# A hybrid decoder layer on one core: decode's weighted sum over value pages moved to TensorE, weight remainders to VectorE, key and value pages in separate rings

## The chip, the core and the metric

The kernel runs on one core of a Trainium2 chip. Its engines run side by side, each in its own program order: TensorE (PE, with its weight loads PEld), VectorE (DVE), ScalarE (ACT), GpSimd (POOL) and SyncE (SP), which here issues most loads. The metric is the device time of one execution in microseconds, the median of several runs; lower is better.

## The reference

One layer of a decoder, for a prompt of 512 tokens (after 16 meta tokens) and 8 decode sequences of one new token each with 2048 past tokens. All of it is fp32.

```
z = rmsnorm(h) @ w_in                       # 2048 -> 8192: hq hf hi hg | aq ak av ag, 8 heads of 128 each
o_hg = hgrn2_chunked(hq, 1-f, hi, log f)    # 8 heads, 128x128 state, chunks of 64; decode: one step on state_hgrn
o_at = diff_attend(aq, ak, av)              # w = softmax(q1 k1) - lam softmax(q2 k2), T5 bias, causal; o = w v
decode: k_past = cache_k[page_table]; v_past = cache_v[page_table]      # 16 pages of 128 tokens per sequence
mixed = concat(rmsnorm(o_hg)*silu(hg), 0.8*rmsnorm(o_at)*silu(ag))
y = rmsnorm(h + mixed @ w_out)              # 2048 -> 2048
```

Outputs are y for prompt and decode tokens, the new keys and values, and the HGRN states. For decode attention each sequence has, per page, 128 tokens by 8 heads by 128 values; `o[h, d]` is the sum over all 2048 tokens of `w[t, h] * v[t, h, d]`.

## The kernel before

**Dense stream.** The two projections are 80 blocks of 128 output features: 64 of `w_in` in the order aq, ak, av, then hi, hf, hq head by head, then the gates hg and ag, and 16 of `w_out` (the blocks o). A block is four groups of four contraction chunks. fp32 is built from two rounded parts: `split` (line 276) makes the high part `hi` of a group's weights on ScalarE and the exact remainder `lo = raw - hi` on POOL, or for some groups on VectorE (`lo_on_dve`, line 291); `group` (line 294) then issues hi x xh, hi x xl and lo x xh for both halves of the columns. The split runs three groups ahead of the products, in rings of four `hi` and four `lo`.

**Order of issue.** Each engine issues in the order of the program's text as it is run in Python (lines 1223 to 1230), and that order is decided there: after each group comes a *slot* (line 1173), in which every chain that can go on issues one stage (`step_threads`): prompt attention, the HGRN heads, the norms, decode's softmax. `fill` (line 559) then adds half passes over decode's pages until VectorE's planned time is a fixed lead ahead of TensorE's (`LATE`: 3.0, 1.5, 4.0 and 4.0 us by phase). The planned times come from `Clock` and `Counted` (lines 74 to 145), rough costs per instruction, among them when a load should have landed.

**Decode attention.** A page is 128 tokens (partitions) by 1024 (8 heads of 128). `page_step` (line 613) does half of a page's pass: for a key page one product with the query row `qb` on all partitions, and a sum over every 64 elements into the scores `scd`; for a value page four of eight products per half, `acc[:, h, :] += v[:, h, :] * w[:, g, h]` (SCALAR_TENSOR_TENSOR, 128x128 each), all on VectorE. Keys run three sequences ahead of values (`KA`), and then key and value pages alternate in one list `steps`, in one ring of six buffers (`pg`) that HGRN's decode state `sd` and values `vb` share. `load_pages` (line 595) issues page loads on SP: it reads the page's number, then starts the DMA, waiting for the buffer. `softmax_dec` (line 657) makes the weights `wd`. `pv_end` (line 694) sums `acc` over the partitions by eight products with a column of ones into `t_o`, and ScalarE copies it to `oSa`.

**End of decode.** Before the last gate block goes on, a loop (lines 1181 to 1185) issues whatever page steps are left.

Of the kernel before, what the change touches and what calls it, by code (L numbers as in the profile page):

```python
# [30 lines left out]
H = 8  # L31
# [6 lines left out]
W = 656                # period of the bias row: a strip's 528 columns and 127 rows  # L38
# [9 lines left out]
def shape_constants():  # L48
    """Matrices that depend on the shapes alone."""
# [8 lines left out]
    # one-hot rows of buckets (row 32: masked) for: the prompt's bias row, decode's far, near and new keys  # L58
# [15 lines left out]
class Clock:  # L74
    """Rough times at which the engines finish what has been issued, for the order of issue."""

    LATENCY = 0.15

    def __init__(self):
        self.now = dict.fromkeys(("pe", "dve", "act", "pool", "dma"), 0.0)  # L80
        self.written, self.read = {}, {}
        self.rings = {}

# [13 lines left out]
    def issue(self, e, cost, outs, ins):  # L97
        start = self.now[e]
        for table, aps in ((self.written, ins + outs), (self.read, outs)):
            for ap in aps:  # L100
                t, by = table.get(ap.tensor.name, (0.0, e))
                if by != e:
                    start = max(start, t + self.LATENCY)
        self.now[e] = end = start + cost
        for ap in ins:
# [5 lines left out]
    def arrive(self, ap, mb):  # L111
        """A load that is issued now."""
# [5 lines left out]
class Counted:  # L118
    """An engine whose instructions' rough times are kept."""
# [4 lines left out]
    def __getattr__(self, op):  # L124
        f = getattr(self.eng, op)

        def call(*a, **k):
# [6 lines left out]
            n = (ins[0] if op == "tensor_reduce" else outs[-1] if "out" not in k else outs[0]).free_size()  # L134
            if self.name == "pe":
                t = 0.11 if op == "transpose" else n / 2400 + 0.004 if ap_dtype(ins[0]) == F32R else 0.2 if n == 1 else max(0.11, n / 600)
            elif self.name == "dve":
                t = 0.065 + n / 960 + (0.06 if op in ("scalar_tensor_tensor", "tensor_tensor_reduce") else 0)
            elif self.name == "act":
                t = 0.07 + n / 1200  # L140
            else:
                t = n / 410
            self.clock.issue(self.name, t, outs, ins)
            return r
        return call

# [6 lines left out]
def layer_kernel(ctx: ExitStack, tc: tile.TileContext, A):  # L153
# [20 lines left out]
    def expln():  # L174
        """The table with both the exponential and the logarithm."""
# [53 lines left out]
    def keep_warm(n):  # L229
        """Products that nobody reads, for TensorE's clock."""  # L230
# [13 lines left out]
    blocks = []                 # (name, weights, halves of columns)  # L244
# [17 lines left out]
    LASTP = ((0, 256), (256, CQ))       # the last block in parts, so that little is left to store at the end  # L262
# [5 lines left out]
    def load_raw(i):  # L268
        """Half of a block's weights."""
# [6 lines left out]
    def split(u):  # L276
        """High part of a group of weights, rounded to float32r, and the exact rest."""
# [8 lines left out]
        (V if lo_on_dve(b, g) else G).tensor_tensor(lo, raw, hi.bitcast(F32), op=ALU.subtract)  # L286
# [3 lines left out]

    def lo_on_dve(b, g):
        return b == 1 or (0 < b < 8 and g % 2 == 0) or (b >= NIN and g == 1)
# [55 lines left out]
    # the norm's weights to every partition; to columns for the meta and decode tokens  # L348
# [34 lines left out]
    # the first block's first half runs while the rest of the prompt is transposed  # L383
# [46 lines left out]
    # the small parameters  # L430
# [34 lines left out]
    def small_constants():  # L465
# [15 lines left out]
        # the prompt's bias by distance, negated: a row per head, skewed through DRAM into a strip per head  # L481
# [31 lines left out]
    aq = mp.tile([P, H, CQ], F32, name="aq")            # -q/8, then the attention half of mixed  # L513
    ak = [None] * H
    hgm = [None] * H                                      # the HGRN half of mixed
# [9 lines left out]
    ktail = [cp.tile([P, 2 * NM], F32, name=f"kt{i}") for i in range(2)]     # the last keys of a head, its two parts apart  # L525
# [4 lines left out]
    # Each group of the dense product is followed by one stage of every chain that can go on; decode  # L530
    # attention's passes over pages fill VectorE up to the time that TensorE has reached.
# [27 lines left out]
    def fill():  # L559
        """Passes over pages until VectorE's work reaches to TensorE's present time."""  # L560
        ph = 0 if "av0" not in flags else 1 if "attn7" not in flags else 2 if "hgrn7" not in flags else 3
        while clock["dve"] < clock["pe"] + LATE[ph]:
            i = done[0]
            if i < len(loaded) and clock.written[loaded[i].tensor.name][0] > clock["pe"] + SOON:
# [4 lines left out]
    def later(slots, **k):  # L569
        """A store some slots from now, so that its queue's engine needn't wait."""  # L570
# [14 lines left out]
    for s in range(NS):  # L585
        ks = [("k", s + KA, g) for g in range(NPG)] if s + KA < NS else []
        vs = [("v", s, g) for g in range(NPG)]
        if s:
            steps += ks[:2] + [x for i in range(NPG) for x in vs[i:i + 1] + ks[i + 2:i + 3]]
        else:  # L590
            steps += vs[:2] + [x for i in range(NPG) for x in ks[i:i + 1] + vs[i + 2:i + 3]]
    loaded = []
    done = [0]

    def load_pages(upto):
        while len(loaded) < min(upto, len(steps)):
            kind, s, g = steps[len(loaded)]
            i = s * NPG + g
            t = pg.tile([P, H * P], F32, name="pgt", tag="pg", bufs=NPB)
            r = nc.sync.value_load(ptab[0:1, i:i + 1], min_val=0, max_val=NPHYS - 1)  # L600
            load(out=t, in_=(ck if kind == "k" else cv)[bass.ds(r, 1), :, :].rearrange("o t c -> (o t) c"))
            loaded.append(t)
            clock.arrive(t, 0.5)
# [3 lines left out]
    def load_q(s):  # L607
        if s < NS:
            qbs[s] = pg.tile([P, H * P], F32, name="qb", tag="acc" if s == 1 else "qb")
# [3 lines left out]
    def page_step():  # L613
        """Half of a page's pass."""
        i = done[0]
        if i >= len(steps):
            return False
        kind, s, g = steps[i]
        z = half[0]
        if z == 0:  # L620
            if kind == "k" and (flags.get("q", slot[0]) >= slot[0] or g == 0 and s >= KA and f"w{s - KA}" not in flags):
                return False
            if kind == "v" and (f"w{s}" not in flags or g == 0 and s and flags.get(f"pv{s - 1}", slot[0]) >= slot[0]):
                return False
            load_pages(i + 1)
            if g == 0 and kind == "k":
                scs[s] = sm.tile([P, NPG + 1, 2 * H], F32, name="scd", bufs=KA)
            elif g == 0:
                accs[s] = pg.tile([P, H, P], F32, name="acc", tag="acc")
        pt = loaded[i]  # L630
        if kind == "k":
            if z == 0:
                V.tensor_tensor(pt, pt, qbs[s], op=ALU.mult)
            else:
                V.tensor_reduce(scs[s][:, g, :], pt.rearrange("p (a d) -> p a d", d=64), axis=AX.X, op=ALU.add)
        else:
            acc, w = accs[s], ws[s]
            vt = pt.rearrange("p (h d) -> p h d", d=P)
            for h in range(z * H // 2, (z + 1) * H // 2):
                if g == 0:  # L640
                    V.tensor_scalar(acc[:, h, :], vt[:, h, :], w[:, g, h:h + 1], None, op0=ALU.mult)
                else:
# [614 lines left out]
```

## Time and profile before

| | us |
|---|---|
| median of 3 runs | 1352.16 (1349.47 to 1352.70) |
| span of the profiled execution, first to last instruction | 1346.6 |
| TensorE busy | 1218.8 (91%) |
| VectorE busy | 946.8 (70%) |
| POOL busy | 590.0 (44%) |
| ScalarE busy | 545.0 (40%) |
| DMA moved | 261 MB, 194 GB/s on average |

The page gives the profiled execution's span alone; the three runs were timed 2.9 to 6.1 us above it. Dense products are short and follow each other closely, and an instruction's duration holds the time through the array, so the sum of durations in a group of matmuls is more than the time they take up. All instructions issued through the planner's wrapper have the line of that wrapper (L128), so groups are told apart by tile names: `lo<-raw,hi` is a weight remainder, `ps` the dense products, `pgt` a page, `acc` the value sum, `ho` and `am` an HGRN head, `sc` attention scores, `t_o` the end of a sequence's value sum.

### The profile page before, as it was taken

What the parts mean: (1) busy time and instruction counts of PE and PEld (TensorE: products, weight loads), DVE (VectorE), ACT (ScalarE), POOL (GpSimd) and SP (SyncE); (2) the same over time, 40 slices, a digit from 0 to 9 for tenths busy, and PEclk for the clock granted to TensorE, in tenths of its full rate; (3) what the DMA queues carried; (4) which work ended last, traced back from release to release, by engine and by line L of the source; (5) the groups of instructions that cost most, each with busy time, mean ns of one, the idle gap of its engine ahead of it and who ended that gap; (6) DMA issues with size and microseconds to landing.
All of it is one profiled execution on the core that took longest, in us unless ns stands there. A gap on an engine that the chain in (4) does not pass through costs nothing. (4 is left out here: it accounts for less than half of the span.)

```text
span 1346.6 us, 25420 instructions
## 1 busy us (share of the span) xinstructions
PE 1218.8 (91%) x9260; PEld 1150.8 (85%) x9260; DVE 946.8 (70%) x1945; ACT 545.0 (40%) x1286; POOL 590.0 (44%) x415
## 2 busy tenths in 40 slices
PE   8999999999999999889979897989973849999995
PEld 6999999887787999789979897889973849999995
DVE  7410899977787879989999999999996544222123
ACT  6322232365566635445535443434310115232233
POOL 3123455422222434345343442534789684344350
PEclk9999999999999999899998998979986969999998
DMA  6453899844544567677786768769676532732323
GB/s 214 121 137 99 304 351 308 281 154 143 150 144 141 187 190 236 217 247 227 233 261 223 241 211 259 237 208 297 205 244 202 179 111 87 232 92 79 95 79 128
DMA packets 240961, 261.05 MB, mean 194 GB/s; under 512 B 8783, under 2 KB 198962, under 8 KB 240171
## 3 DMA queue, kind: packets, MB, share of 16 engines
q1 hardware_dynamic: 57298, 164.09, 36.3%
q10 hardware_dynamic: 183538, 95.34, 25.0%
q8 instruction: 73, 1.20, 0.4%
q14 instruction: 52, 0.43, 0.1%
HBM read 245.94 MB, written 16.14 MB: 195 GB/s over the span
## 5 line engine op out<-in xcount | busy, mean ns | idle before, releaser
L128 POOL TENSOR_TENSOR lo<-raw,hi 128x512 fp32r<-128x512 f32 x288 | 477.3, 1663 | 693.3 <-ACT hi L128 546.6
L128 PE MATMUL ps<-xh,hi 128*128 128x264 f32 (+2 forms) x2048 | 555.3, 300 | 9.1 <-ACT hv L128 5.7
L128 PE MATMUL ps<-xl,hi 128*128 128x264 f32 (+2 forms) x2048 | 535.6, 290 | 1.1 <-DVE xl L128 1.1
L128 PEld LDWEIGHTS ps<-xh,hi 128*128 128x128 f32 x2048 | 398.5, 195 | 26.3 <-issue 9.9
L128 PEld LDWEIGHTS ps<-xl,hi 128*128 128x128 f32 x2048 | 398.6, 195 | 5.2 <-issue 3.8
L128 PE MATMUL ps<-xh,lo 128*128 128x264 f32 (+2 forms) x2048 | 341.6, 290 | 43.5 <-POOL lo L128 43.5
L128 DVE SCALAR_TENSOR_TENSOR acc<-pgt,wd,acc 128x128 f32<-128x128 f32 x960 | 365.9, 452 | 0.0
L128 PEld LDWEIGHTS ps<-xh,lo 128*128 128x128 f32 x2048 | 292.8, 194 | 43.9 <-POOL lo L128 43.9
L128 ACT CAST hi<-raw 128x512 fp32r<-128x512 f32 x321 | 195.4, 616 | 291.2 <-PE ps L128 180.3
L128 DVE TENSOR_TENSOR pgt<-pgt,qb 128x1024 f32<-128x1024 f32 x128 | 172.4, 1347 | 38.4 <-DMA pgt<-in_cache_k 29.8
L128 DVE TENSOR_REDUCE scd<-pgt 128x16 f32<-128x1024 f32 x128 | 155.4, 1214 | 2.3
L128 PE MATMUL ps<-mh,hi 128*128 128x256 f32 (+1 forms) x512 | 130.0, 286 | 3.0 <-ACT gate L128 1.5
L128 PE MATMUL ps<-ml,hi 128*128 128x256 f32 (+1 forms) x512 | 128.5, 283 | 0.0
L128 PEld LDWEIGHTS ps<-mh,hi 128*128 128x128 f32 x512 | 96.4, 188 | 3.9 <-ACT gate L128 1.7
L128 PEld LDWEIGHTS ps<-ml,hi 128*128 128x128 f32 x512 | 96.5, 188 | 0.0
L128 DVE TENSOR_TENSOR lo<-raw,hi 128x512 fp32r<-128x512 f32 x33 | 34.8, 1059 | 79.7 <-ACT hi L128 79.3
L128 DVE TENSOR_TENSOR xr<-xr,t_y 128x512 f32<-128x512 f32 (+1 forms) x17 | 11.2, 656 | 112.3 <-PE t_y L128 112.3
L128 PE MATMUL ps<-mh,lo 128*128 128x256 f32 (+1 forms) x512 | 82.4, 283 | 0.0
L128 PEld LDWEIGHTS ps<-mh,lo 128*128 128x128 f32 x512 | 70.3, 188 | 0.0
L128 DVE SCALAR_TENSOR_TENSOR p<-p,r,p 128x144 f32<-128x144 f32 (+3 forms) x32 | 18.1, 566 | 41.6 <-ACT p L128 41.5
L128 ACT COPY hgm<-ho 128x128 f32<-128x128 f32 x32 | 8.5, 265 | 86.0 <-PE ho L128 86.0
L128 DVE TENSOR_SCALAR acc<-pgt,wd 128x128 f32<-128x128 f32 x64 | 21.4, 402 | 29.2 <-PE t_o L128 29.2
(227 smaller groups left out, 1214.0 us busy)
## 6 DMA issues: line engine op xcount, KB each, us to landing
pgt<-in_cache_k SPq DMA_DIRECT2D x128, 512.0 KB
pgt<-in_cache_v SPq DMA_DIRECT2D x128, 512.0 KB
raw<-in_w_in ACTq DMA_DIRECT2D x125, 512.0 KB
raw<-in_w_out ACTq DMA_DIRECT2D x32, 512.0 KB
x<-in_x_prompt SPq DMA_DIRECT2D x4, 1024.0 KB
qb<-qd SPq DMA_DIRECT2D x8, 512.0 KB
sd<-in_state_hgrn SPq DMA_DIRECT2D x8, 512.0 KB
vb<-hvd SPq DMA_DIRECT2D x8, 512.0 KB
```

What stands on the lines that cost most here:

```text
L128: r = f(*a, **k)
```

## The change

- Every weight remainder `lo` is computed on VectorE.
- The weighted sum over value pages is done by TensorE. A value step takes two pages. Four fp32 products, one for each half of each page, have 32 columns of weights as the stationary operand (the page's 8 heads and those of the pages behind it, of which only the first 8 rows of the result matter) and 512 columns of values as the moving one; they write PSUM partitions 0, 32, 64 and 96 of one bank `t_pv`. VectorE copies the first into `acc` and adds the other seven of a sequence. The wanted values lie in blocks on the diagonal; `pv_end` transposes `acc` in four parts and picks them with a strided read.
- Key pages have a ring of three (`kp`), value pages a ring of two (`pg`), `sd` and `vb` a buffer each. A value step is issued at most once per slot, when the planner thinks that both pages have landed; it then issues the loads of the next two.
- Keys may run two sequences ahead of the softmax and three ahead of the end of values.
- The planner's costs and latencies are others, and it knows a port that POOL and some VectorE instructions hold. Some small tiles share buffers. Comments and docstrings are gone.

```diff
 class Clock:
-    LATENCY = 0.15
+    LATENCY = 0.07
...
+    def port(self, t):
+        for a, b in self.held:
+            if a <= t < b:
+                t = b
+        return t
...
     def split(u):
...
-        (V if lo_on_dve(b, g) else G).tensor_tensor(lo, raw, hi.bitcast(F32), op=ALU.subtract)
+        V.tensor_tensor(lo, raw, hi.bitcast(F32), op=ALU.subtract)
...
-    NPB = 6                     # pages on chip
+    NKB, NPB = 3, 2
...
-    AHEAD = NPB - 1
-    KA = 3                      # sequences by which the keys run ahead of the values
-    steps = [("k", s, g) for s in range(KA) for g in range(NPG)]
...
+    VB = 2
+    NVB = NPG // VB
+    ksteps = [(s, g) for s in range(NS) for g in range(NPG)]
+    vsteps = [(s, n) for s in range(NS) for n in range(NVB)]
...
+    def load_values():
+        n = len(vloaded)
+        if n < len(vsteps):
+            s, m = vsteps[n]
+            vloaded.append([load_page(cv, s * NPG + m * VB + i, "pg", NPB) for i in range(VB)])
...
     def page_step():
...
-            if kind == "k" and (flags.get("q", slot[0]) >= slot[0] or g == 0 and s >= KA and f"w{s - KA}" not in flags):
+            if flags.get("q", slot[0]) >= slot[0] or g == 0 and (s >= 2 and f"w{s - 2}" not in flags or s >= KA and f"pv{s - KA}" not in flags):
                 return False
...
-            for h in range(z * H // 2, (z + 1) * H // 2):
-                if g == 0:
-                    V.tensor_scalar(acc[:, h, :], vt[:, h, :], w[:, g, h:h + 1], None, op0=ALU.mult)
-                else:
-                    V.scalar_tensor_tensor(acc[:, h, :], vt[:, h, :], w[:, g, h:h + 1], acc[:, h, :], op0=ALU.mult, op1=ALU.add)
...
+    def value_step(landed=True):
+        n = vdone[0]
+        if n >= len(vsteps) or n >= len(vloaded):
+            return
+        s, m = vsteps[n]
+        if flags.get(f"w{s}", slot[0]) >= slot[0] or m == 0 and s and flags.get(f"pv{s - 1}", slot[0]) >= slot[0]:
+            return
+        if landed and any(clock.written[t.tensor.name][0] > clock["pe"] for t in vloaded[n]):
+            return
+        po = tp("t_pv")
+        wb = [ws[s][:, m * VB + i:m * VB + i + 32 // H, :].rearrange("p g h -> p (g h)") for i in range(VB)]
+        for r in range(VB // 2):
+            for j in range(4):
+                i = 2 * r + j // 2
+                T.matmul(po[32 * j:32 * j + 32, :], wb[i], vloaded[n][i][:, j % 2 * 512:(j % 2 + 1) * 512],
+                         start=r == 0, stop=r == VB // 2 - 1)
+        if m == 0:
+            accs[s] = pg.tile([P, 512], F32, name="acc", tag="acc")
+            V.tensor_copy(accs[s], po)
+        else:
+            V.tensor_tensor(accs[s], accs[s], po, op=ALU.add)
+        vdone[0] += 1
+        load_values()
+        if m == NVB - 1:
+            spawn(pv_end(s))
...
     def pv_end(s):
...
-        for h in range(H):
-            T.matmul(t[:, h:h + 1], accs[s][:, h, :], ones[:, 0:1], start=True, stop=True)
-        S.copy(oSa[:, s, :], t[:, 0:H])
+        for c in range(4):
+            T.transpose(t[:, c * P:(c + 1) * P], accs[s][:, c * P:(c + 1) * P], ident)
+        parts_ = [bass.AP(tensor=t.tensor, offset=t.offset + o, ap=[list(t.ap[0]), [36, 2], [P + 1, 4]]) for o in (0, 64)]
+        V.tensor_copy(oSa[:, s, :].rearrange("p (a c) -> p a c", c=4), parts_[0])
+        V.tensor_tensor(oSa[:, s, :].rearrange("p (a c) -> p a c", c=4), oSa[:, s, :].rearrange("p (a c) -> p a c", c=4), parts_[1], op=ALU.add)
...
-        sd = pg.tile([P, NS, P], F32, name="sd", tag="pg", bufs=NPB)
+        sd = pg.tile([P, NS, P], F32, name="sd", tag="sd")
...
     for u in range(NG, (NB - 1) * NG):
...
         step_threads()
+        value_step()
         fill()
```

The instructions move as follows. On VectorE in the middle of an HGRN head, before (`am` and `st` are the head's, `pgt` with `scd` a key page, `acc` a value page's eight products):

```order
L128 TENSOR_REDUCE scd<-pgt 128x16
L128 SCALAR_TENSOR_TENSOR acc<-pgt,wd,acc 128x128 x8
L128 TENSOR_TENSOR pgt<-pgt,qb 128x1024
L128 COPY_PREDICATED am_500<-cst,at 128x128
L128 SCALAR_TENSOR_TENSOR st<-st,eb,up 128x128 x2
```

and in the changed program at such a place:

```order
L149 TENSOR_TENSOR lo<-raw,hi 128x512
L149 COPY_PREDICATED am_501<-cst,at 128x128
L149 SCALAR_TENSOR_TENSOR st<-st,eb,up 128x128 x2
L149 TENSOR_TENSOR acc<-acc,t_pv 128x512
L149 TENSOR_TENSOR pgt<-pgt,qb 128x1024
```

The eight products of a value page have gone from between two `am`; a remainder per group and an addition from PSUM per value step stand there.

At the end of decode on VectorE, before (the values of the last two sequences, then decode's norm):

```order
L128 TENSOR_SCALAR acc<-pgt,wd 128x128 x8
L128 SCALAR_TENSOR_TENSOR acc<-pgt,wd,acc 128x128 x120
L128 TENSOR_SCALAR acc<-pgt,wd 128x128 x8
L128 SCALAR_TENSOR_TENSOR acc<-pgt,wd,acc 128x128 x120
L128 TENSOR_TENSOR wnew<-wnew,avS 128x64
```

and in the changed program:

```order
L149 TENSOR_TENSOR lo<-raw,hi 128x512 x3
L149 TENSOR_TENSOR acc<-acc,t_pv 128x512
L149 TENSOR_TENSOR lo<-raw,hi 128x512 x2
L149 COPY oSa<-t_o 128x8
L149 TENSOR_TENSOR oSa<-oSa,t_o 128x8
```

The two runs of 120 products are gone; the last value steps come one every three groups of remainders.

On TensorE, the end of a sequence in an HGRN slot before (`ps` is the dense stream, `at` and `up` the head's):

```order
L128 MATMUL ps<-xh_109,lo 128x264 x4
L128 MATMUL at<-qe,hf 128x128
L128 MATMUL up<-hvtok,hktok 128x128 x2
L128 MATMUL t_o<-ones,acc 128x1 x8
L128 MATMUL ps<-xh_110,hi 128x272
```

and a value step in such a slot of the changed program:

```order
L149 MATMUL ps<-xh_109,lo 128x264 x4
L149 MATMUL at<-qe,hf 128x128
L149 MATMUL up<-hvtok,hktok 128x128 x2
L149 MATMUL t_pv<-pgt,wd 32x512 x4
L149 MATMUL ps<-xh_110,hi 128x272
```

There are 64 such steps, most of them two or three groups apart, the last 81 groups of dense products before the end; the last `t_o` of before stands 70 groups before the end.

## Rows read from the trace of the kernel before

**Rows 1.** The page's busy table and its slices (tenths, 40 slices).

```profile
PE 1218.8 (91%) x9260; PEld 1150.8 (85%) x9260; DVE 946.8 (70%) x1945; ACT 545.0 (40%) x1286; POOL 590.0 (44%) x415
...
PE   8999999999999999889979897989973849999995
```

**Rows 2.** Stages: busy us of each engine, granted clock, DMA share and rate.

```profile
440.00:935.00 495.00, 452.82 (x3389) 430.97 (x3388) 457.90 (x826) 230.22 (x566) 216.33 (x151) 0.94 0.73 231
935.00:1147.00 212.00, 157.20 (x1227) 155.57 (x1225) 143.57 (x447) 51.85 (x100) 156.99 (x69) 0.86 0.58 179
```

**Rows 3.** Waits of TensorE: us in total, times, longest.

```profile
PE ps L128 <- POOL lo L128: 43.5, 2, 22.4
PE ho L128 <- DVE am L128: 27.9, 13, 7.0
PE t_o L128 <- DVE acc L128: 9.6, 3, 7.5
PE t_hkt L128 <- DVE cf L128: 6.1, 3, 2.1
```

**Rows 4.** Timeline of POOL in the decode tail: start, duration, what.

```profile
999.85 32.91 POOL L128 TENSOR_TENSOR lo<-raw,hi 128x512 fp32r<-128x512 f32 x2 [1.83 <-ACT hi L128]
...
1039.72 1.28 POOL L128 TENSOR_TENSOR lo<-raw,hi 128x512 fp32r<-128x512 f32 x1 [1.85 <-ACT hi L128]
```

**Rows 5.** Timeline of VectorE there.

```profile
998.82 31.59 DVE L128 SCALAR_TENSOR_TENSOR acc<-pgt,wd,acc 128x128 f32<-128x128 f32 x120
...
1132.39 0.69 DVE L128 TENSOR_TENSOR lo<-raw,hi 128x512 fp32r<-128x512 f32 x1
```

**Rows 6.** VectorE in an HGRN head, without and with a remainder on POOL.

```profile
535.05 2.18 DVE L128 SCALAR_TENSOR_TENSOR acc<-pgt,wd,acc 128x128 f32<-128x128 f32 x8
...
539.53 3.18 DVE L128 SCALAR_TENSOR_TENSOR acc<-pgt,wd,acc 128x128 f32<-128x128 f32 x8
```

**Rows 7.** Four stretches at the lower clock, columns as in Rows 2.

```profile
1012.20:1036.10 23.90, 4.51 (x21) 4.51 (x22) 18.21 (x70) 1.24 (x2) 23.90 (x6) 0.50 0.71 226
1077.00:1097.50 20.50, 3.22 (x14) 3.22 (x15) 16.10 (x62) 1.14 (x2) 20.50 (x5) 0.50 0.33 104
541.10:551.40 10.30, 7.28 (x32) 6.83 (x33) 9.40 (x24) 2.53 (x8) 1.27 (x1) 0.50 0.67 229
...
821.00:827.80 6.80, 6.80 (x30) 6.35 (x31) 6.56 (x19) 2.54 (x8) 1.27 (x1) 0.50 0.78 275
```

**Rows 8.** Groups: xcount, busy us, mean ns of one, idle before.

```profile
L128 POOL TENSOR_TENSOR lo<-raw,hi 128x512 fp32r<-128x512 f32 x288 | 477.3, 1663 | 693.3 <-ACT hi L128 546.6 <-issue 77.2 <-PE ps L128 30.4
...
L128 DVE SCALAR_TENSOR_TENSOR acc<-pgt,wd,acc 128x128 f32<-128x128 f32 x960 | 365.9, 452 | 0.0
...
L128 DVE TENSOR_TENSOR lo<-raw,hi 128x512 fp32r<-128x512 f32 x33 | 34.8, 1059 | 79.7 <-ACT hi L128 79.3 <-ACT lbe L128 0.3
...
L128 DVE TENSOR_TENSOR xr<-xr,t_y 128x512 f32<-128x512 f32 x15 | 10.3, 688 | 104.5 <-PE t_y L128 104.5
```

**Rows 9.** Timeline of TensorE: scores, a norm's sum, a sequence's end.

```profile
264.09 1.13 PE L128 MATMUL sc<-ak,aq 64*128 64x512 f32 x4
265.14 0.41 PE L128 MATMUL se<-kt,aq 128*128 128x32 f32 x2
...
299.59 1.12 PE L128 MATMUL t_ra<-sq,ones 128*128 128x512 f32 x2
...
466.77 1.70 PE L128 MATMUL t_o<-ones,acc 128*128 128x1 f32 x14
```

**Rows 10.** The chain that ended last, two pieces of the output projection.

```profile
1164.98 0.44 PE t_y L128 x4
1165.52 11.50 PE ps L128 x96
```

**Rows 11.** Timeline of the load queue at the first key pages.

```profile
133.77 23.84 SPq L601 DMA_DIRECT2D pgt<-in_cache_k  x12
```

**Rows 12.** Timeline of VectorE at the first key page.

```profile
140.96 1.22 DVE L128 TENSOR_TENSOR pgt<-pgt,qb 128x1024 f32<-128x1024 f32 x1 [29.25 <-DMA pgt<-in_cache_k]
```

More of the change, by code (lines that the diff above doesn't have):

```diff
@@ L95, in tile, with issue @@
         return t
-    def issue(self, e, cost, outs, ins):
+    def port(self, t):
[3 more added lines that the diff above has]
+        return t
+    def issue(self, e, cost, outs, ins, latency=0.08, shared=False):
         start = self.now[e]
@@ L103, in issue @@
                     start = max(start, t + self.LATENCY)
+        if e == "pool":
+            start = self.port(start)
+            self.pool_held = start + cost
+        elif shared:
+            start = max(start, self.pool_held)
+            a, b = self.held[-1]
+            self.held = self.held[-40:]
+            if start - b < 0.03:
+                self.held[-1] = (a, start + cost)
+            else:
+                self.held.append((start, start + cost))
         self.now[e] = end = start + cost
+        end += latency
         for ap in ins:
@@ L133, in call @@
             ins = aps + [x for n, x in k.items() if hasattr(x, "free_size") and n not in ("out", "accum_out")]
-            n = (ins[0] if op == "tensor_reduce" else outs[-1] if "out" not in k else outs[0]).free_size()
+            n = max(ins[0].free_size(), 1) if op == "tensor_reduce" else (outs[-1] if "out" not in k else outs[0]).free_size()
+            late, shared = 0.08, False
+            from_psum = any(in_psum(x) for x in ins + outs)
+            wide = [x for x in ins if x.free_size() > 1 and not in_psum(x)]
@@ L135, in call @@
             if self.name == "pe":
-                t = 0.11 if op == "transpose" else n / 2400 + 0.004 if ap_dtype(ins[0]) == F32R else 0.2 if n == 1 else max(0.11, n / 600)
-            elif self.name == "dve":
-                t = 0.065 + n / 960 + (0.06 if op in ("scalar_tensor_tensor", "tensor_tensor_reduce") else 0)
+                late = 0.165
+                if op == "transpose":
+                    t = 0.11
+                elif ap_dtype(ins[0]) == F32R:
+                    t = max(0.11, n / 2400 + 0.0115)
+                else:
+                    t = 2 * max(0.118, n / 1200 + min(ins[0].free_size(), P) / 1200)
+                    if ins[0].partition_size() == 64:
+                        t /= 2
+                    if ins[0].free_size() == 32:
+                        t /= 4
+            elif self.name == "dve":
+                two = op in ("scalar_tensor_tensor", "tensor_tensor_reduce")
+                one = op in ("tensor_scalar", "tensor_copy") and not from_psum
+                t = (0.13 if two or op == "tensor_scalar" else 0.075) + n / (1920 if one else 960) * (2 if op == "tensor_tensor_scan" else 1)
+                if op == "tensor_tensor_reduce":
+                    t += 0.13
+                shared = len(wide) >= 2 or one and n > 64
@@ L139, in call @@
             elif self.name == "act":
-                t = 0.07 + n / 1200
+                t = n / 1200 + (0.055 if from_psum else 0.095) + (0.09 if hasattr(k.get("scale"), "free_size") or k.get("accum_out") is not None else 0)
             else:
-                t = n / 410
-            self.clock.issue(self.name, t, outs, ins)
-            return r
-        return call
+                t = 0.07 + n / 430
+            self.clock.issue(self.name, t, outs, ins, late, shared)
+            return r
@@ L148, in ap_dtype, with in_psum @@
+        return call
+def in_psum(ap):
+    return ap.space == bass.MemoryType.PSUM
 def ap_dtype(ap):
@@ L563, in fill @@
             i = done[0]
-            if i < len(loaded) and clock.written[loaded[i].tensor.name][0] > clock["pe"] + SOON:
+            if i < len(kloaded) and any(clock.written[t.tensor.name][0] > clock["pe"] + SOON for t in (kloaded[i], qbs[ksteps[i][0]])):
                 break
@@ L581, in layer_kernel, with load_page, load_keys @@
     scs, qbs, ws, accs = {}, {}, {}, {}
-    AHEAD = NPB - 1
-    KA = 3
-    steps = [("k", s, g) for s in range(KA) for g in range(NPG)]
[L585 to L589, printed above, removed]
-        else:
[L591 to L603, printed above, removed]
+    VB = 2
+    NVB = NPG // VB
+    ksteps = [(s, g) for s in range(NS) for g in range(NPG)]
+    vsteps = [(s, n) for s in range(NS) for n in range(NVB)]
+    kloaded, vloaded = [], []
+    done, vdone = [0], [0]
+    def load_page(src, i, tag, bufs):
+        t = pg.tile([P, H * P], F32, name="pgt", tag=tag, bufs=bufs)
+        r = nc.sync.value_load(ptab[0:1, i:i + 1], min_val=0, max_val=NPHYS - 1)
+        load(out=t, in_=src[bass.ds(r, 1), :, :].rearrange("o t c -> (o t) c"))
+        clock.arrive(t, 0.5)
+        return t
+    def load_keys(upto):
+        while len(kloaded) < min(upto, len(ksteps)):
+            kloaded.append(load_page(ck, len(kloaded), "kp", NKB))
+    def load_values():
[3 more added lines that the diff above has]
+            vloaded.append([load_page(cv, s * NPG + m * VB + i, "pg", NPB) for i in range(VB)])
     half = [0]
@@ L608, in load_q @@
         if s < NS:
-            qbs[s] = pg.tile([P, H * P], F32, name="qb", tag="acc" if s == 1 else "qb")
+            qbs[s] = pg.tile([P, H * P], F32, name="qb", tag="qb")
             clock.arrive(qbs[s], 0.5)
```

69 lines of the change are left out of this document (30 added, 39 removed).

## The prediction

> **What bounds the kernel now.** I read the page's busy table and slices first, then the stages, then TensorE's waits, then the timeline at the longest of them. TensorE is busy for 91% of the span and its slices stand at 8 or 9 but for one dip near the end [rows 1], so the time is TensorE's work, plus the holes in it, plus what its clock loses. The holes are few and have owners: two of 22 us each are TensorE waiting for a weight remainder `lo` from POOL (43.5 in all), and 27.9 + 9.6 + 6.1 = 43.6 us are waits for VectorE's results (`am`, `acc`, `cf`) [rows 3]. They lie where VectorE is fullest: between 440 and 935 us, the HGRN heads, it is busy for 458 of 495 us; the decode tail follows [rows 2].
>
> The two long holes are one mechanism. VectorE runs 120 products of value pages in a row, 31.59 us, and over the same stretch POOL takes 32.91 us for two remainders, of which one takes 1.28 alone [rows 4, 5]. A POOL instruction that reads SBUF does not get in between VectorE instructions with two SBUF inputs. The other way round one remainder on POOL stretches eight such products from 2.18 to 3.18 us [rows 6], and the product of scores, `am`, stands behind them. The Trainium skill (SBUF — State Buffer, Who interferes with whom) has the shared ports taken by whoever issues first, for one whole instruction. By that POOL would lose at most one product, 0.26 us, and the first term below would be nothing (the sum would end at 1375); the rows show a hold through the whole chain, and I go by them.
>
> **The change, term by term**, against the profiled execution's 1346.6 us.
>
> 1. *The two holds by POOL go*: no remainder is left on POOL and no chain of page products on VectorE. 43.5 us of waits [rows 3]. TensorE also ran the first microseconds after each at half clock: 4.5 + 3.2 us of work in the two stretches at 0.50 [rows 7], half of which comes back: 4. What is late next there? Nothing of decode: the changed order has its last value step 81 groups before the end, and the loop that gave VectorE whole sequences at once finds nothing left. Together −47.
>
> 2. *VectorE's load.* Off: 960 products, 365.9 us. On: 288 remainders, at 0.69 us (a lone one, [rows 5]) to 1.06 us (the mean of those it did before, many beside POOL, [rows 8]), 199 to 305 us, and 64 additions of a 128x512 product from PSUM at 0.69 (the residual's form, [rows 8]), 44 us. So VectorE ends 20 to 120 us lighter. This is not on the path itself; it decides how often TensorE still waits for VectorE. Of the 43.6 us I take 70% as gone: `am` no longer stands behind 2.2 to 3.2 us of value products, but it still stands behind key pages. Ends: nothing (VectorE stays full, since the same rule fills it with key pages) and all of it. −30.5.
>
> 3. *The clock.* From 440 to 935 us it is 0.94 on average [rows 2], so about 12% of 495 us, 59 us, is at 0.50, and TensorE works through 82% of such a stretch (14.1 of 17.1 us in the two shown, [rows 7]). That costs 59 x 0.82 / 2 = 24 us. The stretches follow the waits of term 2, so 70% goes with them: −17. Ends: 0 and −24.
>
> 4. *The end of a sequence.* Before: 16 records of one column, 1.70 us for the last 14 [rows 9], 1.9 in all, eight times: 15. Now four transposes and a little, as the residual's (0.44, [rows 10]) with 0.1 for the rest: 4. −11.
>
> 5. *The value steps on TensorE*, 64 of them, each four fp32 products of 128 rows, 32 columns out and 512 moving columns in four column groups. No row shows column groups. The nearest are row groups: two fp32 products of 64 rows and 512 columns each start at 264.09, and what follows them starts at 265.14 [rows 9]: the pair takes 1.05, while one product over 128 rows takes 1.12 with its end. The two halves of the array thus run together. If four column groups do the same, a step is 1.05, plus 0.1 for coming in from the dense shape: 64 x 1.15 = +74. Lower end: the streaming alone, 0.9, is 58. Upper ends: two at a time, 2.1, is +134; one at a time, 4.2, is +269. I take 1.15, by the row nearest to it. The Trainium skill (TensorE: Matmul & The Clock Gate, Measured speedup vs the span model) has three column groups 2.38 times faster than one after another; estimated from that page, a set costs 1.26 of a lone product, 1.3 us by the row, and the sum would be 10 us higher. No run here shows it.
>
> 6. *Value pages arriving.* The two-page ring is loaded again only when a step has read it. By the program's order 36 of 63 distances between steps are two groups, at 2.9 us each (11.50 a block of four, [rows 10]) 5.8 us and whatever other products stand in them. A page took 7.2 us from issue to use with the queue's `qb` loads ahead (133.77 to 140.96, [rows 11, 12]), and pages are issued at most 2.0 apart (23.84 for 12). So two pages take at most 9.2 us, 3.4 too many, 122 us over 36 steps; the lower end is nothing. I take 5: that first page shared the queue, and most distances hold attention or HGRN products besides. Behind a waiting step stands the next dense group; VectorE's addition, and the key pages behind it, wait too.
>
> 7. *The rest.* The first remainders now stand behind the normalisation on VectorE: 0 to 4, I take 2. Recalibrated costs in the planner shift key pages by a step or two: −5 to +5, I take 0. Separate buffers for the HGRN state and POOL's gate products stay off the path: POOL is left with under 120 us.
>
> Sum: −47 − 30.5 − 17 − 11 + 74 + 5 + 2 = −24.5, a span of 1322. The median of the runs, 1352.16, stands 5.6 above the profiled span; with the same 5.6 the forecast is **1328 us**.
>
> **Rivals.**
> - *Everything VectorE delayed goes* (term 2 −43.6, term 3 −24), steps cost 1.05 and pages never wait: −47 − 43.6 − 24 − 11 + 67 = −59, 1294. For it: the chains that made `am` late are gone. Against: the planner still packs VectorE to a fixed lead over TensorE.
> - *VectorE stays the bound in the heads*: a remainder per group plus a key page (2.4) plus its HGRN work and the addition is about 4.8 us, beside a group of 2.9 with the HGRN products and half a value step. Then terms 2 and 3 give nothing: 1328 + 47.5 = 1375. It decides if VectorE is again busy for over nine tenths there.
> - *Column groups do not run together*: slower, 1328 + 60 = 1388 with two at a time, 1523 one at a time. The point from which the change loses is a step of about 1.5 us. For it: no row shows fp32 products in column groups. Against: the row groups do overlap.
> - *Value pages are late*: 2 us on each of the 36 close steps is 72 instead of 5: 1395, slower.
>
> **How the numbers follow.** Forecast 0.58 (its own range 1304 to 1348); everything goes 0.12; VectorE the bound 0.12; column groups apart 0.11; pages late 0.07. What a measurement here can tell from no change is about 0.3%, so faster is below 1348 and slower above 1356. Faster: 0.54 + 0.12 + 0.04 from the milder half of the VectorE case = 0.70. Same: 0.03 + 0.04 = 0.07. Slower: 0.23. The range 1288 to 1386 leaves out the last two rivals' upper parts (0.14) and a little below the best case (0.04).
>
> **What would show it.** The waits of TensorE for POOL's `lo` are gone and none for VectorE's `lo` has come in their place (if one has, term 2 was wrong). A value step takes 1.0 to 1.3 us from its first product to the next dense one, and its four groups start together; 2 us or more means they do not overlap. VectorE is busy for 65 to 85% in the heads, the clock there is 0.97 or better, and waits for `am` are under 12 us. Waits of `t_pv` for `pgt` are under 10 us in all. The time after the last value step is as before, some 12 us a block. The prediction is wrong if TensorE's waits stay near 110 us, or if the value steps add over 100.

## The result and the profile after

| | before | after |
|---|---|---|
| median, four runs each, side by side | 1350.82 us (1347.66 to 1352.70) | 1287.91 us (1287.09 to 1291.81) |
| ratio, 95% interval | | 0.9547 [0.9526, 0.9567] |
| profiled span | 1346.6 us | 1285.5 us |

The change makes the kernel 4.5% faster, more than twice the gain forecast (1328 us), and the time lies just below the range, which began at 1288. The direction was right. One term failed in its size and in its reason, a second was too small because of it, and a third was missing.

The busy table and the slices of the kernel after, to be held against [rows 1]:

```profile
PE 1249.9 (97%) x9676; PEld 1122.7 (87%) x9676; DVE 788.9 (61%) x1289; ACT 547.3 (43%) x1278; POOL 124.7 (10%) x135
...
PE   8999999999999999999998999999999999999995
```

TensorE's time outside busy was 1346.6 - 1218.8 = 127.8 us and is now 1285.5 - 1249.9 = 35.6: 92.2 us less. Its busy time rose by 31.1. The span's change is just these two, -92.2 + 31.1 = -61.1. The dip near the end of the slices has gone.

Two stages of the kernel after, in the columns of [rows 2]: the HGRN heads, and the rest of decode.

```profile
440.00:900.00 460.00, 449.90 (x3462) 390.74 (x3461) 353.06 (x499) 222.48 (x551) 63.64 (x41) 0.98 0.81 265
900.00:1085.00 185.00, 185.00 (x1509) 170.73 (x1508) 85.19 (x135) 66.00 (x118) 24.94 (x27) 1.00 0.56 175
```

VectorE is busy for 77% of the heads instead of 93%, and TensorE for 98% instead of 91%; the granted clock there is 0.98 instead of 0.94. Behind the heads TensorE has no hole at all. Over the whole span the mean granted clock rose from 0.951 to 0.989 (one view, of the kernel before and of the kernel after):

```profile
core 0: 1346.6 us, clock 0.951
```

```profile
core 0: 1285.5 us, clock 0.989
```

TensorE's longest waits in the kernel after, to be held against [rows 3]:

```profile
PE t_x L149 <- DVE x L149: 3.8, 5, 1.3
PE t_pv L149 <- DVE wd L149: 3.7, 1, 3.7
PE t_pv L149 <- DMA pgt<-in_cache_v: 3.0, 3, 1.9
PE t_w L149 <- ACT vtok L149: 2.1, 6, 0.3
PE t_pv L149 <- DVE st L149: 1.6, 2, 1.0
PE t_pv L149 <- ACT wmT L149: 1.2, 2, 0.6
```

Not one of the four waits of [rows 3] is among them, and no remainder of VectorE's has taken their place. In TensorE's timeline, a passage from one dense group to the next without a value step, one with a step, and the longest wait in front of a step (the records of a fp32 product count double, so x8 is four products):

```profile
1002.84 0.65 PE L149 MATMUL ps<-xh,lo 128*128 128x264 f32 x4
...
1003.44 0.28 PE L149 MATMUL ps<-xl,hi 128*128 128x256 f32 x1
...
1005.73 0.65 PE L149 MATMUL ps<-xh,lo 128*128 128x264 f32 x4
1006.31 1.06 PE L149 MATMUL t_pv<-pgt,wd 128*32 128x512 f32 x8
1007.30 0.39 PE L149 MATMUL ps<-xh,hi 128*128 128x256 f32 x1
1007.53 0.28 PE L149 MATMUL ps<-xl,hi 128*128 128x256 f32 x1
...
698.92 1.94 PE L149 MATMUL t_pv<-pgt,wd 128*32 128x512 f32 x8 [3.66 <-DVE wd L149]
```

From its start to the next dense product the step takes 0.99 us; over the 64 steps the median is 1.00. That is not all it costs: from `ps<-xh,lo` to `ps<-xl,hi` it is 0.60 us without a step and 1.80 with one, so the step puts 1.20 us into the stream. (The median over the 20 steps that stand between two dense groups is 1.20, too.) The groups that answer to [rows 8]:

```profile
L149 DVE TENSOR_TENSOR lo<-raw,hi 128x512 fp32r<-128x512 f32 x321 | 248.0, 776 | 241.8 <-ACT hi L149 241.7
L149 PE MATMUL t_pv<-pgt,wd 128*32 128x512 f32 x512 | 74.1, 614 | 10.5 <-DVE wd L149 3.7 <-DMA pgt<-in_cache_v 3.0 <-DVE st L149 1.6
L149 DVE TENSOR_TENSOR acc<-acc,t_pv 128x512 f32<-128x512 f32 x56 | 38.2, 683 | 57.8 <-PE t_pv L149 57.8
L149 PE MATMUL t_o<-ident,acc 128*128 128x128 f32 x32 | 5.1, 280 | 0.6 <-DVE st L149 0.6
```

A remainder on VectorE costs 776 ns, near the lower bound taken for it. `t_pv` adds 74.1 us to TensorE's busy time and `t_o` takes 12.6 off (17.7 before). What is left of the +31.1 is -30.4: the other products did not become fewer, they run at the full clock for longer. In the stretches at 0.50 TensorE was busy for 78.4 us before and is for 16.1 now; half of the difference is 31 us.

### The profile page after: what moved, and what is told of

It reads as the page before. It is cut to its first block, busy times and chain, and to the rows that moved or that the text cites. A ratio compares the mean times of both kernels' runs of the same rounds, so it can differ in the third digit from the quotient of the medians.

```text
span 1285.5 us, 25160 instructions
## 1 busy us (share of the span) xinstructions
PE 1249.9 (97%) x9676; PEld 1122.7 (87%) x9676; DVE 788.9 (61%) x1289; ACT 547.3 (43%) x1278; POOL 124.7 (10%) x135
## 4 chain that ended last, share of the span: by engine, by line
PE 89%; DMA 3%; DVE 3%; ACT 2%; issue 1%; ACTq 1%; SPq 0%; DVEq 0%
PE ps L149 70%; PE t_pv L149 5%; PE o L149 2%; DMA pgt<-in_cache_v 2%; PE sc L149 2%; PE ho L149 2%; DMA raw<-in_w_out 1%; PE t_w L149 1%; PE t_os L149 1%; PE up L149 1%; PE at L149 1%; PE t_ra L149 1%; PE t_y L149 1%; PE t_rh L149 0%; DVE x L149 0%
## 5 line engine op out<-in xcount | busy, mean ns | idle before, releaser
L149 PE MATMUL ps<-xh,hi 128*128 128x264 f32 (+2 forms) x2048 | 543.5, 295 | 0.0
L149 PE MATMUL ps<-xl,hi 128*128 128x264 f32 (+2 forms) x2048 | 524.9, 286 | 1.1 <-DVE xl L149 1.1
L149 PEld LDWEIGHTS ps<-xh,hi 128*128 128x128 f32 x2048 | 389.2, 190 | 63.7 <-issue 53.9
L149 DVE TENSOR_TENSOR lo<-raw,hi 128x512 fp32r<-128x512 f32 x321 | 248.0, 776 | 241.8 <-ACT hi L149 241.7
L149 PEld LDWEIGHTS ps<-xl,hi 128*128 128x128 f32 x2048 | 389.3, 190 | 3.6 <-issue 3.5
L149 DVE TENSOR_TENSOR pgt<-pgt,qb 128x1024 f32<-128x1024 f32 x128 | 164.8, 1287 | 8.1 <-DMA pgt<-in_cache_k 6.8
L149 PE MATMUL ps<-ml,hi 128*128 128x256 f32 (+1 forms) x512 | 128.4, 283 | 0.0
L149 PE MATMUL t_pv<-pgt,wd 128*32 128x512 f32 x512 | 74.1, 614 | 10.5 <-DVE wd L149 3.7
L149 DVE TENSOR_TENSOR acc<-acc,t_pv 128x512 f32<-128x512 f32 x56 | 38.2, 683 | 57.8 <-PE t_pv L149 57.8
L149 POOL TENSOR_TENSOR sd<-sd,vb 128x1024 f32<-128x1024 f32 x8 | 20.1, 2509 | 190.3 <-ACT vb L149 162.5
L149 ACT ACTIVATE p<-p,nm 128x144 f32<-128x144 f32 (+3 forms) x64 | 36.2, 565 | 0.7 <-DVE nm L149 0.7
```

The lines of the kernel that those rows point to most:

```text
L149: r = f(*a, **k)
```

## Experiments

The theory behind the forecast: POOL's remainders starve behind chains of page products (the two long holes), and `am` is late because VectorE is full. The rival: `am` is late because POOL and VectorE hold each other up, however full VectorE is, so that one of the three parts of the change (values to TensorE, remainders to VectorE, planner costs) would be enough. Each ratio below is to the kernel before on the same chip, with its 95% interval.

**Remainders alone to VectorE.** The kernel before, with

```diff
     def lo_on_dve(b, g):
-        return b == 1 or (0 < b < 8 and g % 2 == 0) or (b >= NIN and g == 1)
+        return True
```

> The kernel before with every weight remainder on VectorE; values stay there too, the planner is the old one. Theory A (the gain came because the value products left VectorE): VectorE is already busy 458 of 495 us in the heads, 109 more remainders at 0.69 us are 75 us there, so the two holds by POOL go (-47) but TensorE waits for VectorE far more: 1350 to 1430 us, slower than or level with before (1351). Theory C (POOL's remainders were the trouble, by the port they share with VectorE): 1290 to 1310.

Measured: 1323.30 us, ratio 0.980 [0.9778, 0.9822], span 1321.1. That is neither number. Its stages (columns as above; the heads, and the end of decode) and two of TensorE's waits:

```profile
440.00:935.00 495.00, 489.44 (x3879) 471.69 (x3878) 455.96 (x948) 245.68 (x589) 82.94 (x52) 0.99 0.77 240
990.00:1105.00 115.00, 18.21 (x93) 17.55 (x94) 104.83 (x400) 5.87 (x15) 0.25 (x2) 0.53 0.64 199
```

```profile
PE t_o L128 <- DVE acc L128: 89.0, 4, 31.5
...
PE ho L128 <- DVE am L128: 3.7, 3, 2.3
```

In the heads VectorE is as full as before (456 of 495 us, 458 before), yet TensorE waits 3.7 us for `am` instead of 27.9 and runs through. So fullness alone did not make `am` late. What stood in front of it is different: between the first and the last `am` there are 360 value products here and 448 before. The gain there is paid back: the value products that found no room in the heads stand at the end of decode, where TensorE is busy for 18 of 115 us. The same products were also faster without remainders on POOL, 360 ns instead of 452 [rows 8]:

```profile
L128 DVE SCALAR_TENSOR_TENSOR acc<-pgt,wd,acc 128x128 f32<-128x128 f32 x960 | 273.8, 360 | 0.0
```

**The planner's costs alone.** The kernel before with the new `Clock` and `Counted`; the core of the edit is

```diff
-    def issue(self, e, cost, outs, ins):
+    def issue(self, e, cost, outs, ins, latency=0.08, shared=False):
...
+        if e == "pool":
+            start = self.port(start)
+            self.pool_held = start + cost
+        elif shared:
+            start = max(start, self.pool_held)
```

> The kernel before with the changed planner costs alone (Clock and Counted of the changed kernel). Theory A: the holds by POOL stay (43 us of waits for lo) and so does VectorE's load: 1335 to 1355. Theory B (the waits for VectorE went because the planner now knows its times): waits for am, acc and cf fall from 43.6 to under 10 us and the time is 1300 to 1325.

Measured: 1392.65 us, ratio 1.0319 [1.0294, 1.0345]: slower, where both theories had it the same or faster. Its waits of TensorE:

```profile
PE t_o L149 <- DVE acc L149: 95.5, 3, 32.6
PE t_mx L149 <- DVE mx L149: 43.4, 1, 43.4
PE ps L149 <- ACT gate L149: 9.7, 4, 3.7
...
PE ho L149 <- DVE am L149: 4.8, 2, 3.0
```

The planner now knows that the two engines hold each other up, and puts fewer page passes beside the dense stream; the waits for `lo` and nearly all for `am` go, but of the 1024 value products 655 come behind the 200th of the 320 groups of the dense stream, where the kernel before has 455 and the experiment above 592. In the heads they are as slow as before (554 ns on average, 520 before) but fewer: 324 between the first and the last `am`, 448 before. What finds no room comes at the end, in the open.

**Values and remainders moved, with the old planner.** The kernel after, with `Clock` and `Counted` of before and one cost added, for the products of 32 columns:

```diff
+                t = 0.11 if op == "transpose" else n / 2400 + 0.004 if ap_dtype(ins[0]) == F32R else 0.2 if n == 1 else max(0.11, n / 600) / (4 if ins[0].free_size() == 32 else 1)
```

> The changed kernel with the old planner costs (the only addition: a product with 32 output columns is planned at a quarter of its cost). Theory A: VectorE's relief does not depend on the planner, 1288 to 1300. Theory B: waits for VectorE come back, 1315 to 1335.

Measured: 1277.51 us, ratio 0.9449 [0.943, 0.9468]: the fastest of all, below both kernels. The planner's new costs are no part of the gain. Its waits:

```profile
PE t_pv L128 <- ACT wmT L128: 1.3, 2, 0.7
PE t_pv L128 <- DVE st L128: 1.2, 2, 0.7
PE t_pv L128 <- DVE wd L128: 1.2, 1, 1.2
...
PE t_pv L128 <- DMA pgt<-in_cache_v: 1.0, 2, 0.6
```

With other due times the value steps stand where weights and pages are ready: 4.7 us of waits here, 9.5 in the rows of after. Against the kernel after the span is 7.9 us shorter, 4.8 of it idle time and 3.1 busy time.

**Values moved, remainders left on POOL.** The kernel after, with

```diff
-        V.tensor_tensor(lo, raw, hi.bitcast(F32), op=ALU.subtract)
+        on_dve = b == 1 or (0 < b < 8 and g % 2 == 0) or (b >= NIN and g == 1)
+        (V if on_dve else G).tensor_tensor(lo, raw, hi.bitcast(F32), op=ALU.subtract)
```

> The changed kernel with the remainders on POOL for the groups that had them there before. Theory A: no chain of two-input products on VectorE is longer than two, so POOL is never held for long: 1285 to 1300, no wait of TensorE for lo over 3 us. Theory C: the remainders on POOL bring back stretched VectorE work and waits, 1315 to 1340.

Measured: 1284.32 us, ratio 0.9499 [0.9482, 0.9517], with 0.2 us of TensorE's waits for remainders. The group:

```profile
L149 POOL TENSOR_TENSOR lo<-raw,hi 128x512 fp32r<-128x512 f32 x288 | 406.4, 1415 | 691.1 <-ACT hi L149 590.8 <-PE ps L149 29.0 <-issue 26.6
```

A remainder on POOL takes 1415 ns here, 1663 before [rows 8]. The median is 1.29 us in both; the means differ by a few remainders, of which the longest took 31.68 us before and takes 2.39 here. Without the chains of page products POOL is quick enough, and where the remainders are computed no longer matters much.

**The two together.** The old planner and remainders on POOL, both edits above.

> The changed kernel with the old planner costs (as in the third experiment) and the remainders on POOL as before (as in the fourth). Each of the two alone was level or faster; if they add, 1270 to 1276; if the old planner can't place remainders on POOL, waits for lo and am come back, 1285 or more.

Measured: 1295.60 us, ratio 0.9576 [0.9528, 0.9624]. The two do not add. The largest waits are new ones, small and scattered:

```profile
PE ps L128 <- ACT ak L128: 9.5, 4, 5.1
PE t_pv L128 <- issue: 4.7, 1, 4.7
```

**No value products.** The kernel before, without the products of 14 of a sequence's 16 value pages:

```diff
-                else:
+                elif g == NPG - 1:
```

> The kernel before, remainders on POOL and old planner, with the value products of the first and last page of a sequence only (14 of 16 pages are loaded and left out of the sum). If the value products on VectorE are the one cause of the holes (the two long ones, the waits for am, acc and cf) and of the clock's losses, it is 1225 to 1250 us: the changed kernel less its 70 us of value steps, with under 15 us of TensorE's waits for VectorE and POOL. If VectorE's load or POOL's remainders alone make the waits for am, these stay near 28 us and the time is 1265 or more.

Measured: 1220.86 us, ratio 0.9027 [0.8986, 0.9068]. POOL keeps its remainders and the planner is the old one; the page's engines and slices, and the group of remainders:

```profile
PE 1185.8 (97%) x9260; PEld 1123.7 (92%) x9260; DVE 640.5 (53%) x1049; ACT 543.7 (45%) x1284; POOL 529.0 (43%) x415
...
PE   8999999999999999999999999999999999999995
```

```profile
L128 POOL TENSOR_TENSOR lo<-raw,hi 128x512 fp32r<-128x512 f32 x288 | 410.9, 1432 | 639.7 <-ACT hi L128 528.0 <-issue 39.5 <-PE ps L128 22.3
```

TensorE idles for 34.0 us (127.8 before), as in the kernel after. So the long holes and the waits for `am`, `cf` and `hv` had the value products on VectorE as a common condition, and the new rings of pages were not needed to be rid of them: this run has the ring of before. Of the 32 `am` 16 still stand directly behind a key page's product (20 before), and its list of TensorE's waits, down to 0.2 us, has none for `am`. The run also gives a rough bound on what the move could bring, were the new work on TensorE free: 1221; the change as a whole stands 67 us above it.

**What a value step costs without the column groups.** The kernel after, with four products of 128 columns one after another, and then with products of 64 columns, two groups at a time:

```diff
-                T.matmul(po[32 * j:32 * j + 32, :], wb[i], vloaded[n][i][...],
+                T.matmul(po, ws[s][:, 0:NPG, :].rearrange("p g h -> p (g h)"), vloaded[n][i][...],
...
+                T.matmul(po[64 * (j % 2):64 * (j % 2) + 64, :], ws[s][:, 0:NPG // 2, :].rearrange("p g h -> p (g h)"), vloaded[n][i][...],
```

> The changed kernel, but each of the four products of a value step has 128 columns of weights and writes all 128 partitions, so that they can't run beside each other (they overwrite each other and take the weights of the first 16 pages: the decode attention is not computed). If the column groups are what makes a step cheap, a step takes 3.4 to 3.8 us instead of 1.0, 155 to 180 us more over 64 steps: 1440 to 1470, slower than before (1351). If the step was cheap for another reason: under 1310.

> The same with 64 columns of weights, two column groups at a time (the decode attention is not computed here either). A step is 1.8 to 2.0 us: 1335 to 1355, level with before. This is the point from which I said the change would lose; if the extra time on TensorE falls into holes instead, it is under 1320.

Measured: 1422.47 us, ratio 1.0525 [1.0465, 1.0585], one after another, and 1334.71, ratio 0.9876 [0.9819, 0.9933], in pairs. A step in each, in TensorE's timeline; first one after another:

```profile
347.82 3.68 PE L149 MATMUL t_pv<-pgt,wd 128*128 128x512 f32 x8
350.94 0.69 PE L149 MATMUL ps<-xh,hi 128*128 128x272 f32 x1
```

and in pairs:

```profile
329.37 1.94 PE L149 MATMUL t_pv<-pgt,wd 128*64 128x512 f32 x8
331.24 0.39 PE L149 MATMUL ps<-xh,hi 128*128 128x272 f32 x1
```

To the next product these take 3.12 (median 3.13) and 1.87 us, against 0.99 with four groups. Put between two dense groups, they add 3.43 and 2.07 us, against 1.20, all measured from `ps<-xh,lo` to `ps<-xl,hi` as above. The groups' busy times are 235.6, 128.4 and 74.1 us:

```profile
L149 PE MATMUL t_pv<-pgt,wd 128*128 128x512 f32 x512 | 235.6, 603 | 7.2 <-ACT wmT L149 4.2 <-DVE st L149 2.4 <-DMA pgt<-in_cache_v 0.6
```

```profile
L149 PE MATMUL t_pv<-pgt,wd 128*64 128x512 f32 x512 | 128.4, 619 | 10.6 <-ACT wmT L149 3.8 <-DMA pgt<-in_cache_v 3.8 <-DVE st L149 2.0
```

Against the kernel after the spans grow by 134.2 and 46.5 us, the busy times by 161.5 and 54.3, and the steps by 64 x 2.23 = 143 and 64 x 0.87 = 56: most of every microsecond of a step is on the path. One after another, 4 us of the rest are less idle time (31.6 us, 35.6 in the kernel after), and the granted clock is higher, 0.995 instead of 0.989. The expectation for it had the step right, 3.4 us, but took a step of the kernel after as 1.0 us instead of 1.20, so it came out too high. Without column groups the move would have lost; in pairs it still wins 1.2% (two runs each).

**Remainders and planner together, values left on VectorE.** This fills the last corner of the table; the kernel before with the first two edits.

> The kernel before with both the remainders on VectorE (alone: 1323) and the changed planner costs (alone: 1393), values still on VectorE. If the planner costs harm because they place fewer passes beside the dense stream and leave more value products for the end, where TensorE waits for them, remainders on VectorE leave still less room: 1390 to 1430, with over 140 us of waits for acc at the end. If the harm came from POOL's remainders under the new order, it goes with them: under 1335.

Measured: 1335.68 us, ratio 0.9882 [0.9831, 0.9933], just above the second expectation and far below the first.

```profile
PE t_o L149 <- DVE acc L149: 95.5, 3, 32.6
PE t_mx L149 <- DVE mx L149: 6.8, 1, 6.8
```

The wait for the last sequences' values is as long as with the planner alone; the 43.4 us for `mx` are 6.8. The medians of all eight corners:

| | old planner | new planner |
|---|---|---|
| values on VectorE, `lo` on POOL | 1351 (before) | 1393 |
| values on VectorE, `lo` on VectorE | 1323 | 1336 |
| values on TensorE, `lo` on POOL | 1296 | 1284 |
| values on TensorE, `lo` on VectorE | 1278 | 1288 (after) |

Moving the values brings 46 to 108 us in every pair. The new rings and buffers of the pages moved with the values in all of these runs and were not tried by themselves. Moving the remainders brings 18 to 57 in three pairs and nothing in the fourth (4 us the other way; the runs overlap). The planner's costs bring 11 us in one pair and cost 10, 12 and 42 in the others. The change's gain of 63 is the first, with little from the second, and the third took some back.

## Why the prediction was right in direction and too small

By its own terms, each with what the two traces show:

| term | forecast, us | measured, us |
|---|---|---|
| 1. two holds by POOL | -43.5 | -43.5, no wait for `lo` is left |
| 2. TensorE's waits for VectorE | -30.5 | about -43, of 43.6 |
| waits for ScalarE's `hv`, `ak`, `gate`, `y` | not counted | about -11 |
| 1 and 3. clock | -21 | -30 |
| 4. end of a sequence | -11 | -12.6 busy |
| 5. value steps | +74 | +74.1 busy; 64 x 1.20 = 77 put into the stream |
| 6 and 7. pages late, the rest | +7 | about +10, the waits of `t_pv` |

The four rows of idle time (1 and 2, ScalarE, 6 and 7) make -88 of the -92.2; the other 4 are waits of 2 us and less each. Forecast and measured span are 36.6 us apart: term 2 makes 12.5 of them, the waits for ScalarE 11 and the clock, which came back behind the waits, 9.

- *Term 1* held in its size, and in its reason for the two long holes: of the two remainders of [rows 4] the first took 31.68 us, until the chain of products had ended. In the two experiments in which the chains are gone and POOL keeps its work no remainder takes longer than 2.39 us, and TensorE waits 0.2 us for them at most. But the sentence that POOL does not get in between such products is too strong. In the kernel before 66 remainders started on POOL between two of them. 57 got in at once: they took 1.27 to 1.48 us, and the product that gave way 1.35 to 1.52 us instead of 0.34. Eight stood at least until the chain had ended, three of these behind 52 to 116 products for 15.0, 31.7 and 29.6 us (the remaining one took 1.51). One that got in:

```profile
810.90 3.21 DVE L128 SCALAR_TENSOR_TENSOR acc<-pgt,wd,acc 128x128 f32<-128x128 f32 x8
...
811.88 1.29 POOL L128 TENSOR_TENSOR lo<-raw,hi 128x512 fp32r<-128x512 f32 x1 [5.27 <-ACT hi L128]
```

The Trainium skill (SBUF — State Buffer, Who interferes with whom) gives the shared ports to whoever issues first, for that whole instruction, and blocks the other. The 57 agree with it; the eight, which stood for more than one instruction, do not. Why these eight lost is open.
- *Term 2 is the step that failed*, in its share and in its reason. "Of the 43.6 us I take 70% as gone", because `am` would still stand behind key pages on a full VectorE. None of the three waits is left in a list that goes down to 0.6 us. The reason falls with the first experiment, VectorE as full as before and 3.7 us of waits for `am`, and with the one without value products, where key pages still stand in front of `am` and it is not waited for. What stood in front of the late ones was a value chain: in 11 of the 13 waits for `am`, 26.1 of the 27.9 us, eight value products and one key product lie right before it on VectorE. Nine of these chains had work of POOL beside them and took 3.18 to 6.45 us; the other two took 2.18 and 2.19. The bound "all of it" stood in the text, as the first rival's: that rival's 1294 was nearest, and its 0.12 was too little. How much of this is the slowing and how much the number and place of the chains is left open, but the second counts: the waits also fell, to 4.8 us, with the new planner, which keeps POOL's remainders and products as slow, but puts fewer of them into the heads (324 instead of 448).
- *A term was missing.* About 11 us of TensorE's waits were put down to ScalarE (5.7 for `hv`, 2.7 for `ak`, 2.2 for `gate`, 0.9 for `y`). The prediction does not name them. None of them is left in the list of after. The largest, for `hv`, was by the profile's release a delay of VectorE at one remove (last section). Those for `ak` and `y` do not all hang on the value products: without these, 2.2 and 1.1 us of them are still there.
- *Term 3* had the right mechanism. The granted clock fell to 0.50 in waits or behind them (the stretch from 541.1 us [rows 7] begins in the wait of 7.0 us for `am` that ended at 544.1), and with more of these gone than forecast, more came back: 30 us, where the text's own upper end with term 1 was 28.
- *Term 5* was right by the row it chose, within 3 us: a step puts 1.20 us into the stream, against 1.15. Two at a time is 2.07 us, where the bound was 2.1, and one at a time 3.43, below its 4.2. The Trainium skill (TensorE: Matmul & The Clock Gate, Measured speedup vs the span model) has 2.38 for three column groups; the 1.3 us estimated from that page were 0.1 too many. The runs here have 3.43 / 1.20 = 2.9 for four groups, against products of full width; none has three.
- *Term 6* held: 3.0 us for value pages, in three waits, against 5. The two-page ring is no bound. The wait of 3.66 us for `wd` was not foreseen; it is a step issued before the softmax was through.
- *Term 7* took the planner's costs at zero within 5 us. By the table they cost 10 (1288 against 1278), and 42 with the other parts undone. That was the most mis-sized of the small terms, and the total does not show it.
- *The offset* was 5.6 us; the median after stands 2.4 above the profiled span, and the profiled run itself, timed at 1287.33, 1.8. That is 3 us of the miss.

The busy-share test in "what would show it" came out as written (77%, between 65 and 85), and for a reason that the experiments do not support: 92% in the first experiment would have failed it, with 3.7 us of waits for `am`.

What stays open: why the planner's costs hurt by 42 us with everything else as before. The rows show where (43.4 us for `mx`, 95.5 for the last values), and that fewer value passes stood beside the dense stream. That its costs for the shared port are to blame, and not those for other instructions, was not tried.

## What to carry to other kernels

A busy share says that an engine may be late, not that it is: look at the instruction in front of the late one, and at what lengthens it. When one cause (here chains of products on a shared engine) stands behind several waits, count all waits that may hang on it, those put down to a third engine too, and look at what stands in front of each before you discount it. Parts of a change that help apart can undo each other, so the planner that issues them is an edit of its own and wants its own run.

## What the runs showed of the hardware that was not expected

**Four column groups of fp32 products run wholly together.** In 56 of the 64 steps of the kernel after, the four products of the first pass start within 20 ns (0, 7, 13 and 20), and those of the second pass 0.453 us later, just as close. The two passes are 0.91 us of the 1.20 that a step puts into the dense stream, so going into this shape and back costs about 0.29 us. Weight loads of 32 columns are shorter, too:

```profile
L149 PEld LDWEIGHTS ps<-xh,hi 128*128 128x128 f32 x2048 | 389.2, 190 | 63.7 <-issue 53.9 <-ACT hi L149 5.9 <-ACT scd L149 0.6
...
L149 PEld LDWEIGHTS t_pv<-pgt,wd 128*32 128x32 f32 x512 | 11.0, 108 | 27.3 <-issue 4.2 <-DMA pgt<-in_cache_v 3.9 <-DVE wd L149 3.9
```

**A load for one engine seems to have held up another engine's load.** In the kernel before, TensorE waited for ScalarE's `hv`, and ScalarE stood still in front of a weight load that it issues itself (L274). All engines' timeline there:

```profile
586.05 2.47 SPq L601 DMA_DIRECT2D pgt<-in_cache_k  x2
...
589.75 0.38 ACTq L274 DMA_DIRECT2D raw<-in_w_in  x1
590.17 0.68 ACT L128 ACTIVATE hv<-ps 128x272 f32<-128x272 f32 x2 [5.42 <-DMA pgt<-in_cache_k]
...
590.62 0.39 PE L128 MATMUL ps<-xh,hi 128*128 128x264 f32 x1 [2.08 <-ACT hv L128]
```

The activation needs no page. By the profile it was released by a key page's landing, whose load SP had issued at 586.05, when VectorE had freed its buffer; it stands behind ScalarE's weight load in that engine's order, and so came 5.4 us late, and TensorE 2.1 us. That the two loads share a semaphore is inferred from the release, and was not tested. In the kernel after, the list of TensorE's waits has none for `hv`. By this reading a late VectorE had reached TensorE by way of SP and ScalarE.
